# Gated recurrence of a hybrid trunk layer: score products of 32 columns, state products of 64 value columns, one output bank for two heads

## The chip, the core and the metric

The kernel runs on one core of a Trainium2 chip. The core's engines run side by side, each through its own list of instructions in order: PE (TensorE, matrix products; its weight loads are listed as PEld), DVE (VectorE), ACT (ScalarE), POOL (GpSimd) and SP, which issues the DMAs. The metric is the device time of one execution in microseconds (us). The time before is 3231.66 us, the median of three runs (3231.03 to 3231.88).

## What is computed

One layer: an RMS norm, a combined input projection, a gated linear recurrence (branch A), a pooling branch (branch B), their gated merge, an output projection, and a gated MLP. There are 2048 tokens behind 16 meta tokens, 1024 features and 8 heads; a head has 128 key features and 64 value features. All of it is float32. The change touches the recurrence alone:

```python
def hgrn2_mixer(q, f_logit, i, og, lb, head_g):
    """S_t = diag(f_t) S_{t-1} + (1 - f_t) i_t^T ; o_t = S_t^T q_t   (per head, S in R^{A_KDIM x A_VDIM})."""
    ...
    f = lbf + (1.0 - lbf) * jax.nn.sigmoid(f_logit.astype(f32))
    k = 1.0 - f
    ...
        o_inter = jnp.einsum('bhtk,bhkv->bhtv', q_ * jnp.exp(a_), S)
        scores = jnp.einsum('bhtsk,bhsk->bhts', q_[:, :, :, None, :] * decay, k_)
        o = o_inter + jnp.einsum('bhts,bhsv->bhtv', scores, v_)
        S = jnp.exp(a_last[:, :, 0, :])[..., None] * S + jnp.einsum(
            'bhsk,bhsv->bhkv', k_ * jnp.exp(a_last - a_), v_)
```

The kernel uses chunks of 128 tokens instead of the 64 of this code; the results are the same function.

## The kernel before

The tokens are taken in four segments of 512; the first has the 16 meta tokens ahead. A segment runs through the recurrence, the pooling branch, the norm factors of the heads, the out gate, the merge, the output projection, the second norm and the MLP. Weights come from memory in pieces of 512 KB; ACT (L85) and DVE (L86) split each piece into two parts, and a projection (`proj`, L108) makes three products of every 128 features with them, 24 products of up to 512 columns for one block of 128 output features.

The recurrence goes over four pairs of heads (`for p in range(PAIRS)`). For a pair, both heads lie side by side in the tiles `f`, `k` and `q` (features on partitions, tokens along the columns). Four projections fill them: two for `f` (sigmoid on ACT, L479 and L480, then `k` by L482), two for `q` (ACT L488, DVE L489). `decays` (DVE, L259, L273, L279) makes products of `f` within blocks of eight tokens. `all_scores` then fills the causal score tiles `at`, one per head, level by level: within blocks of 8, then between the halves of blocks of 16, 32, 64 and 128 tokens (`h_` = 0, 8, 16, 32, 64). Ahead of every level DVE multiplies `q` and `k` by decays, so PE, which reads both, has to be done with a level before DVE goes on to the next, and PE has to wait for DVE before it starts that one.

The three low levels (`h_` below 32) are whole products of 128 keys by 128 queries per chunk and head (L296), four chunks to a bank `sp`. Levels 0 and 8 are taken out of the bank by DVE with a mask, `copy_predicated` (L303), level 16 by ACT in four small copies per head (L300). Levels 32 and 64 (L309) compute only the needed blocks, 32 by 32 and 64 by 64, and ACT copies them (L312). At level 32 each head's products are written in the order `for o in range(0, C, 2 * h_): for c in range(n)`: four with their output on partitions 0 to 31, then four on partitions 64 to 95. The partitions of the output are the columns of the PE array that a product uses, and its column group is meant by that below.

`chunks_out` (per head) transposes the four chunks of `k` (L361, bank `ktp`; ACT copies to `kt`, L363), makes the state products (L366, bank `up`: weights `kt`, moving the 128 value columns of the pair, of which the head needs 64), updates the states on DVE (L372, L384), and sums scores times values (L378) and queries times state (L380) in bank `op`, all 128 value columns for each head; ACT copies the head's 64 rows out (L386). All banks of this part (`sp`, `ktp`, `up`, `op`) share three PSUM buffers (tag `hg`).

A scheduler sets the order of each engine's list ahead of time. It has placed products of the next pair's projections (L108) between the levels of the present pair, to fill the time in which DVE works on `q` and `k`. A fp32 product of the recurrence is listed in the trace as two records of weight load and product; L108, whose operands are split, has one record per product.

Of the kernel before, what the change touches and what calls it, by code (L numbers as in the profile page):

```python
# [16 lines left out]
P = 128  # L17
D = 1024
KB = D // P
META = 16  # L20
# [16 lines left out]
LEVELS = (8,)  # L37
# [7 lines left out]
def trunk_layer(ctx: ExitStack, tc: tile.TileContext, x, meta, wts, cst, gf, wpool, out):  # L45
# [14 lines left out]
    # ---------------------------------------------------------------- first loads  # L60
# [14 lines left out]
    # ---------------------------------------------------------------- helpers  # L75
    nxt = [0]

    def weights(lo=None):
        """the next piece of the weight stream, split exactly into two float32r parts"""
        i = nxt[0]  # L80
        nxt[0] += 1
        raw = wpl.tile([P, 1024], F32, name="raw", bufs=RAW)
        nc.sync.dma_start(out=raw, in_=wts[i])
        w = wpl.tile([P, 2, 1024], F32R, name="w")
        A.copy(out=w[:, 0, :], in_=raw)  # L85
        (lo or V).tensor_tensor(out=w[:, 1, :], in0=raw, in1=w[:, 0, :].bitcast(F32), op=ALU.subtract)  # L86
        return w

    def split(dst, src, scale=None):
        """dst[:,0] + dst[:,1] == src * scale"""  # L90
# [10 lines left out]
    def proj(w, kof, nk, src, c0, parts):  # L101
        """feature-major product: out[128 features, tokens]; one bank per part"""
# [11 lines left out]
    def rows_one_by_one(src, chunks, nk, consume):  # L114
        """the same with all weights held and chunk after chunk finished"""
# [10 lines left out]
    def rows_product(src, chunks, nk, consume, between=(), lo=None):  # L126
        """token-major product: out[tokens, 512]; the weights come in pieces of two k blocks"""
# [15 lines left out]
    def rsqrt(dst, src, t1, t2):  # L143
        """dst = (src) ** -0.5; src, t1, t2 in SBUF, float32; dst, t1, t2 written"""
# [7 lines left out]
    def square_sums(acc, src, m):  # L152
        """acc[:m, 0] = the sums of squares along src's rows of 512"""
# [3 lines left out]
    def inv_rms(ss, n):  # L157
        """ss [P, 2, n]: sums of squares of two half rows; returns [P, n], 1 / rms of the row"""
# [13 lines left out]
    def transposed(rows, sizes, offs, dst, gbase):  # L172
        """dst[kb] = the rows' block kb transposed, times its norm weight, split"""
# [36 lines left out]
    def norm1_first(xt, sizes, offs):  # L210
        """the first segment's, in two batches of rows"""
# [19 lines left out]
    def norm1(s):  # L231
        """closures, one per chunk of segment s, and the tiles that they fill"""
# [28 lines left out]
    def decays(f, N):  # L261
        """what the decays of blocks of eight need: the products around the middle of a block, their inverses"""
# [24 lines left out]
    def scores(q, k, geo, h_):  # L287
        """the scores between the halves of blocks of 2 h_ tokens (h_ 0: within blocks of eight)"""
        for (off, n, C, a_t) in geo:
            if h_ >= C:  # L290
                continue
            qv, kv = q[:, off:off + n * C], k[:, off:off + n * C]
            sp = ps.tile([P, 512], F32, name="sp", tag="hg", bufs=HG)
            if h_ < 32:
                for c in range(n):
                    T.matmul(sp[:C, c * C:(c + 1) * C], lhsT=kv[:, c * C:(c + 1) * C], rhs=qv[:, c * C:(c + 1) * C],  # L296
                             start=True, stop=True)
                if h_ == 16:
                    for o in range(0, C, 2 * h_):
                        A.copy(out=a_t[o:o + h_, :, o + h_:o + 2 * h_],  # L300
                               in_=sp[o:o + h_, :n * C].rearrange("p (c t) -> p c t", t=C)[:, :, o + h_:o + 2 * h_])
                    continue
                V.copy_predicated(out=a_t.rearrange("p c t -> p (c t)"),  # L303
                                  mask=masks[h_][:C, :n, :C].rearrange("p c t -> p (c t)"), data=sp[:C, :n * C])
                continue
            for o in range(0, C, 2 * h_):
                for c in range(n):
                    b = c * C + o
                    T.matmul(sp[o:o + h_, c * h_:(c + 1) * h_], lhsT=kv[:, b:b + h_], rhs=qv[:, b + h_:b + 2 * h_],  # L309
                             start=True, stop=True)  # L310
            for o in range(0, C, 2 * h_):
                A.copy(out=a_t[o:o + h_, :, o + h_:o + 2 * h_],  # L312
                       in_=sp[o:o + h_, :n * h_].rearrange("p (c t) -> p c t", t=h_))
# [40 lines left out]
    def chunks_out(h, q, k, tot, off, n, C, a_t, vt, first, o_raw, W):  # L354
        """the outputs of n chunks of C tokens at column off for head h, and the states between them"""
        p, r = h // 2, h % 2
        N = n * C
        qv, kv = q[:, off:off + N], k[:, off:off + N]
        ktp = ps.tile([P, 512], F32, name="ktp", tag="hg", bufs=HG)
        for c in range(n):  # L360
            T.transpose(out=ktp[:C, c * P:(c + 1) * P], in_=kv[:, c * C:(c + 1) * C], identity=ident)  # L361
        kt = tpl.tile([P, 512], F32, name="kt", tag="t")
        A.copy(out=kt[:C, :n * P], in_=ktp[:C, :n * P])  # L363
        up = ps.tile([P, 512], F32, name="up", tag="hg", bufs=HG)
        for c in range(n):
            T.matmul(up[:, c * P:(c + 1) * P], lhsT=kt[:C, c * P:(c + 1) * P], rhs=vt[c][:C, p * P:(p + 1) * P],  # L366
                     start=True, stop=True)
        if n > 1:
            sc = tpl.tile([P, 3, P], F32, name="sc", tag="t")
        states = [st[:, h, :]]  # L370
# [387 lines left out]
```

## Time and profile before

| what | value |
|---|---|
| median of 3 runs | 3231.66 us |
| profiled execution, span from first to last instruction | 3224.6 us |
| PE busy | 3162.8 us (98%) |
| DVE busy | 1761.0 us (55%) |
| ACT busy | 1154.1 us (36%) |
| products of the low score levels (L296, 128 columns) | 768 records, 101.1 us |
| products of levels 32 and 64 (L309) | 768 records, 34.6 us |
| granted TensorE clock, mean | 0.995 |

The span is the time from the first to the last instruction of the profiled execution; the median of the runs is 7.1 us longer. Busy times are sums over the whole span. Records of PE overlap each other (the mean record of L296 lasts 286 ns, but the next one starts after some 0.11 us), so what a group of products costs is read from the starts of what stands before and behind it. Where an engine stands idle ahead of an instruction, the trace gives the time in square brackets with what ended it.

### The profile page before, as it was taken

The page shows a single profiled execution, that of the slowest core. Times are in us where ns is not written, and L with a number is a line of the kernel's source. Part 1 is how long each engine was busy: PE and PEld are TensorE (multiplying, and loading weights), DVE is VectorE, ACT ScalarE, POOL GpSimd, SP SyncE. Part 2 cuts the span into 40 slices and gives each one's busy share as a digit, 9 for nine tenths or more (in the row PEclk, how much of TensorE's full clock was granted, in tenths as well). Part 3 has the DMA queues.
Part 4 walks back from the last instruction along what each step waited for, and adds up shares of the span by engine and source line. Part 5 has one row for each costly group of instructions (what it writes and reads, how often), then busy time and mean ns, then how long its engine had stood idle before and what let it go on. Part 6 is the DMA issues. An engine that isn't in the chain of part 4 may idle for free.

```text
span 3224.6 us, 41323 instructions
## 1 busy us (share of the span) xinstructions
PE 3162.8 (98%) x16748; PEld 2640.0 (82%) x16748; DVE 1761.0 (55%) x2959; ACT 1154.1 (36%) x1897; POOL 51.2 (2%) x183
## 2 busy tenths in 40 slices
PE   7999999999999999999999999999999999999998
PEld 6999978898878788888877778888888878878887
DVE  5776355454477636445457754654456783354545
ACT  4333244242333325323333433532333342232323
POOL 1000000000000000000000000000000000000000
PEclk9999999999999999999999999999999999999999
DMA  4112232222331223222241122322223112222222
GB/s 149 53 54 79 86 105 92 92 92 95 101 111 60 73 97 118 92 92 98 91 150 60 53 90 95 110 98 92 98 99 124 53 59 95 95 80 97 95 95 85
DMA packets 81730, 294.58 MB, mean 91 GB/s; under 512 B 9074, under 2 KB 9202, under 8 KB 81540
## 3 DMA queue, kind: packets, MB, share of 16 engines
q1 hardware_dynamic: 81540, 291.95, 27.1%
q8 instruction: 131, 2.15, 0.3%
q14 instruction: 59, 0.48, 0.0%
HBM read 283.52 MB, written 8.39 MB: 91 GB/s over the span
## 4 chain that ended last, share of the span: by engine, by line
PE 92%; DVE 6%; ACT 1%; issue 0%; DMA 0%; SPq 0%; DVEq 0%; ACTq 0%
PE pt L108 60%; PE rp L137 23%; PE sp L296 3%; DVE q L259 1%; DVE scr L259 1%; PE up L366 1%; PE tp L185 1%; DVE k L259 1%; PE sp L309 1%; PE op L380 1%; PE op L378 1%; DVE w L86 1%; PE ktp L361 0%; DVE q L489 0%; PE pp L504 0%
## 5 line engine op out<-in xcount | busy, mean ns | idle before, releaser
L108 PE MATMUL pt<-z,w 128*128 128x512 f32 (+3 forms) x9552 | 1945.8, 362 | 0.0
L108 PEld LDWEIGHTS pt<-z,w 128*128 128x128 f32 x9552 | 1594.1, 188 | 291.6 <-issue 7.5
L86 DVE TENSOR_TENSOR w<-raw,w 128x1024 fp32r<-128x1024 f32 x500 | 612.2, 1224 | 1070.2 <-ACT w L85 1063.5
L85 ACT CAST w<-raw 128x1024 fp32r<-128x1024 f32 x504 | 528.1, 1048 | 753.9 <-PE rp L137 358.7
L137 PE MATMUL rp<-w,act 128*128 128x512 f32 x2040 | 474.4, 394 | 0.0
L137 PEld LDWEIGHTS rp<-w,act 128*128 128x128 f32 x2040 | 383.4, 188 | 89.1
L137 PE MATMUL rp<-w,mix 128*128 128x512 f32 (+1 forms) x816 | 192.7, 395 | 0.0
L639 ACT COPY ub<-pt 128x512 f32<-128x512 f32 (+1 forms) x110 | 55.4, 503 | 354.8 <-PE pt L108 354.8
L137 PEld LDWEIGHTS rp<-w,mix 128*128 128x128 f32 (+1 forms) x816 | 147.6, 182 | 39.3 <-issue 3.5
L646 DVE SCALAR_TENSOR_TENSOR cv<-ub,cs,cv 128x512 f32<-128x512 f32 x176 | 131.7, 748 | 3.1
L581 ACT ACTIVATE sg<-pt 128x512 f32<-128x512 f32 (+1 forms) x80 | 41.2, 515 | 242.2 <-PE pt L108 242.2
L296 PE MATMUL sp<-q,k 128*128 128x128 f32 (+1 forms) x800 | 102.6, 282 | 24.2 <-DVE q L259 24.2
L296 PEld LDWEIGHTS sp<-q,k 128*128 128x128 f32 (+1 forms) x800 | 95.2, 194 | 36.1 <-issue 32.2
L649 ACT ACTIVATE sg<-cv 128x512 f32<-128x512 f32 x88 | 55.6, 632 | 178.5 <-DVE cv L646 178.5
L137 PE MATMUL rp<-w,z 128*128 128x512 f32 (+1 forms) x408 | 102.1, 402 | 0.0
L108 PE MATMUL pt<-oa,w 128*128 128x512 f32 (+2 forms) x480 | 95.0, 349 | 0.0
L108 PE MATMUL pt<-ob,w 128*128 128x512 f32 (+2 forms) x480 | 95.0, 349 | 0.0
L650 DVE TENSOR_TENSOR cv<-cv,sg 128x512 f32<-128x512 f32 x88 | 61.0, 693 | 61.5 <-ACT sg L649 61.5
L137 PEld LDWEIGHTS rp<-w,z 128*128 128x128 f32 (+1 forms) x408 | 73.8, 183 | 18.3 <-issue 0.4
L108 PEld LDWEIGHTS pt<-oa,w 128*128 128x128 f32 x480 | 77.9, 189 | 12.5
L108 PEld LDWEIGHTS pt<-ob,w 128*128 128x128 f32 x480 | 77.8, 189 | 12.5
L681 DVE TENSOR_TENSOR h<-h,rp 128x512 f32<-128x512 f32 x96 | 66.0, 688 | 29.1 <-PE rp L137 26.7
(159 smaller groups left out, 2107.6 us busy)
## 6 DMA issues: line engine op xcount, KB each, us to landing
raw<-in_wts_dram SPq DMA_DIRECT2D x504, 512.0 KB, 3.3
xt<-in_x_dram SPq DMA_DIRECT2D x16, 512.0 KB, 4.4
h<-in_x_dram SPq DMA_DIRECT2D x16, 512.0 KB, 4.5
out_dram<-h SPq DMA_DIRECT2D x12, 512.0 KB, 2.8
gfb<-in_gf_dram SPq DMA_DIRECT2D x8, 256.0 KB, 4.3
out_dram<-h SPq DMA_DIRECT2D x8, 256.0 KB, 2.0
wp<-in_wpool_dram SPq DMA_DIRECT2D x1, 256.0 KB
cs<-in_cst_dram SPq DMA_DIRECT2D x1, 68.0 KB, 6.8
```

The costliest lines, as they stand in the source:

```text
L85: A.copy(out=w[:, 0, :], in_=raw)
L86: (lo or V).tensor_tensor(out=w[:, 1, :], in0=raw, in1=w[:, 0, :].bitcast(F32), op=ALU.subtract)
L108: T.matmul(pt[:, :n], lhsT=w[:, wi, (kof + k) * P:(kof + k + 1) * P], rhs=src[k][:, xi, c0 + o:c0 + o + n], start=(k == 0 and i == 0), sto ...
L137: T.matmul(banks[ci][:n, :], lhsT=src[k][:, xi, o:o + n], rhs=w[:, wi, (k % 2) * 512:(k % 2 + 1) * 512], start=(k == 0 and i == 0), stop=( ...
L259: mul = lambda o, a, b: V.tensor_tensor(out=o, in0=a, in1=b, op=ALU.mult)
L296: T.matmul(sp[:C, c * C:(c + 1) * C], lhsT=kv[:, c * C:(c + 1) * C], rhs=qv[:, c * C:(c + 1) * C], start=True, stop=True)
L581: A.activation(out=sg[:, o:o + n], in_=pt[:, :n], func=AF.Sigmoid)
L639: A.copy(out=ub[:, 2 - e0 + o:2 - e0 + o + n], in_=pt[:, :n])
L646: V.scalar_tensor_tensor(out=cv, in0=ub[:, t_:t_ + SEG], scalar=col(C_CW + t_ * NF, j), in1=cv, op0=ALU.mult, op1=ALU.add)
L649: A.activation(out=sg, in_=cv, func=AF.Sigmoid)
L650: V.tensor_tensor(out=cv, in0=cv, in1=sg, op=ALU.mult)
L681: V.tensor_tensor(out=v, in0=v, in1=bank, op=ALU.add)
```

## The change

Level 16 joins the levels that go through a mask, and all three low levels are computed as blocks of 32 keys by 32 queries only (`B = 32`), of both heads into one bank: 32 products per level and pair, written so that consecutive products go to output partitions 0, 32, 64 and 96 in turn. DVE copies each level by its mask into a new tile `bt` that holds only the diagonal blocks (256 columns for the pair); behind level 16, ACT moves `bt` into `at` in four copies. Levels 32 and 64 also put both heads in one bank, with the chunk loop outside the block loop, and half as many ACT copies of twice the size.

`chunks_out` now takes a pair: both heads are transposed first, the state products have 64 moving columns and share one bank, the states are kept 64 columns wide, and the outputs of head 0 and head 1 go to partitions 0 to 63 and 64 to 127 of one bank, with weights of 64 columns; one ACT copy takes the whole bank. `at` has one tile per pair. The set-up makes three masks of 256 columns per partition instead of two of 512.

```diff
-LEVELS = (8,)
+LEVELS = (8, 16)
...
     def scores(q, k, geo, h_):
-        for (off, n, C, a_t) in geo:
+        for (off, n, C, W, a_t, b_t) in geo:
...
             if h_ < 32:
-                for c in range(n):
-                    T.matmul(sp[:C, c * C:(c + 1) * C], lhsT=kv[:, c * C:(c + 1) * C], rhs=qv[:, c * C:(c + 1) * C],
-                             start=True, stop=True)
-                if h_ == 16:
-                    for o in range(0, C, 2 * h_):
-                        A.copy(out=a_t[o:o + h_, :, o + h_:o + 2 * h_],
-                               in_=sp[o:o + h_, :n * C].rearrange("p (c t) -> p c t", t=C)[:, :, o + h_:o + 2 * h_])
-                    continue
-                V.copy_predicated(out=a_t.rearrange("p c t -> p (c t)"),
-                                  mask=masks[h_][:C, :n, :C].rearrange("p c t -> p (c t)"), data=sp[:C, :n * C])
-                continue
+                B = min(C, 32)
+                spv = sp[:C, :2 * n * B].rearrange("p (e c t) -> p e c t", e=2, c=n)
+                for e in range(2):
+                    for c in range(n):
+                        for o in range(0, C, B):
+                            x = slice(e * W + off + c * C + o, e * W + off + c * C + o + B)
+                            T.matmul(spv[o:o + B, e, c, :], lhsT=k[:, x], rhs=q[:, x], start=True, stop=True)
+                V.copy_predicated(out=b_t, mask=masks[h_, C], data=sp[:C, :2 * n * B])
+                if h_ == 16:
+                    for o in range(0, C, B):
+                        A.copy(out=a_t[o:o + B].rearrange("p e c t -> p (e c) t")[:, :, o:o + B],
+                               in_=b_t[o:o + B].rearrange("p (c t) -> p c t", t=B))
+                continue
+            spv = sp[:, :2 * n * h_].rearrange("p (e c t) -> p e c t", e=2, c=n)
+            for e in range(2):
+                for c in range(n):
+                    for o in range(0, C, 2 * h_):
+                        x = e * W + off + c * C + o
+                        T.matmul(spv[o:o + h_, e, c, :], lhsT=k[:, x:x + h_], rhs=q[:, x + h_:x + 2 * h_],
+                                 start=True, stop=True)
...
-    def chunks_out(h, q, k, tot, off, n, C, a_t, vt, first, o_raw, W):
+    def chunks_out(p, q, k, tot, geo, vt, first, o_raw):
...
+        for e in range(2):
+            v0 = p * P + e * VD
+            for c in range(n):
+                T.matmul(upv[:, e, c, :], lhsT=kts[e][:C, c * P:(c + 1) * P], rhs=vt[c][:C, v0:v0 + VD],
+                         start=True, stop=True)
...
         for c in range(n):
-            o_ = op[:, c * C:(c + 1) * C]
-            T.matmul(o_, lhsT=vt[c][:C, p * P:(p + 1) * P], rhs=a_t[:, c, :], start=True, stop=first)
+            for e in range(2):
+                v0 = p * P + e * VD
+                T.matmul(op[e * VD:(e + 1) * VD, c * C:(c + 1) * C], lhsT=vt[c][:C, v0:v0 + VD],
+                         rhs=a_t[:, e, c, :], start=True, stop=first)
             if not first:
-                T.matmul(o_, lhsT=states[c], rhs=qv[:, c * C:(c + 1) * C], start=False, stop=True)
+                for e in range(2):
+                    x = e * W + off + c * C
+                    T.matmul(op[e * VD:(e + 1) * VD, c * C:(c + 1) * C], lhsT=states[e][c], rhs=q[:, x:x + C],
+                             start=False, stop=True)
...
-        A.copy(out=o_raw[r * VD:(r + 1) * VD, off - r * W:off - r * W + N], in_=op[r * VD:(r + 1) * VD, :N])
+        A.copy(out=o_raw[:, off:off + N], in_=op[:, :N])
```

The scheduler's order moves with it. PE, first pair of the second segment, from level 16 to level 32, before:

```order
L296 MATMUL sp<-q,k 128x128 x8
L108 MATMUL pt<-z_4422,w 128x512
L108 MATMUL pt<-z_4423,w 128x512 x3
L108 MATMUL pt<-z_4424,w 128x512 x3
L309 MATMUL sp<-q,k 32x32 x16
```

and now (L300 are the 32 by 32 products of the low levels, L312 those of levels 32 and 64):

```order
L300 MATMUL sp<-q,k 32x32 x32
L108 MATMUL pt<-z_4625,w 128x512
L108 MATMUL pt<-z_4626,w 128x512 x3
L108 MATMUL pt<-z_4627,w 128x512 x3
L108 MATMUL pt<-z_4628,w 128x512
L312 MATMUL sp<-q,k 32x32 x16
```

Eight products of 128 by 128 have become 32 of 32 by 32, and eight projection products stand behind them instead of seven. PE, the same pair, from the transposes to the outputs, before (the second head follows in the same way):

```order
L361 MATMUL ktp<-ident,k 128x128 x4
L108 MATMUL pt<-z_4422,w 128x512 x3
L108 MATMUL pt<-z_4423,w 128x512
L366 MATMUL up<-vt,kt 128x128 x4
L378 MATMUL op<-at_465,vt 128x128
L380 MATMUL op<-q,st 128x128
L378 MATMUL op<-at_465,vt 128x128
L380 MATMUL op<-q,sc 128x128
```

and now (L366 the transposes, L375 the state products, L389 and L394 the outputs):

```order
L366 MATMUL ktp<-ident,k 128x128 x8
L108 MATMUL pt<-z_4625,w 128x512
L375 MATMUL up<-vt,kt 128x64 x8
L389 MATMUL op<-at_478,vt 64x128 x2
L394 MATMUL op<-q,st 64x128 x2
L389 MATMUL op<-at_478,vt 64x128 x2
L394 MATMUL op<-q,sc 64x128 x2
```

Both heads go through each step together; the outputs are twice as many products of half the weight columns, four per chunk. ACT, the same place and on to the next pair's `f` and `q`, before:

```order
L363 COPY kt<-ktp 128x512
L386 COPY oraw<-op 64x512
L363 COPY kt<-ktp 128x512
L479 ACTIVATE f<-pt,cs 128x512 x2
L480 ACTIVATE f<-f,lb 128x512 x2
L482 ACTIVATE k<-f,one 128x1024
L386 COPY oraw<-op 64x512
```

and now (L368 the copy of the transposes, L402 the copy of the outputs, L503 to L506 `f` and `k`):

```order
L368 COPY kt<-ktp 128x512 x2
L402 COPY oraw<-op 128x512
L503 ACTIVATE f<-pt,cs 128x512 x2
L504 ACTIVATE f<-f,lb 128x512 x2
L85 CAST w<-raw 128x1024
L506 ACTIVATE k<-f,one 128x1024
```

The next pair's `f` now stands behind the copy of both heads' outputs, where it stood behind that of the first head.

## Rows read from the trace of the kernel before

**Rows 1.** The page: busy times of the engines, and the chain's share by engine.

```profile
PE 3162.8 (98%) x16748; PEld 2640.0 (82%) x16748; DVE 1761.0 (55%) x2959; ACT 1154.1 (36%) x1897; POOL 51.2 (2%) x183
PE 92%; DVE 6%; ACT 1%; issue 0%; DMA 0%; SPq 0%; DVEq 0%; ACTq 0%
```

**Rows 2.** Busy time by stretch: length, PE, PEld, DVE, ACT, POOL, clock, DMA, GB/s.

```profile
880.00:1075.00 195.00, 187.43 (x1146) 154.40 (x1145) 145.77 (x292) 75.48 (x147) 3.31 (x8) 0.98 0.23 80
940.00:980.00 40.00, 36.96 (x242) 31.04 (x241) 31.91 (x71) 14.29 (x29) 0.00 (x0) 0.96 0.20 67
```

**Rows 3.** Waits, whole span: total us, times, longest.

```profile
PE sp L296 <- DVE q L259: 24.2, 16, 2.3
```

**Rows 4.** PE in time order, first pair of segment 2: start, length, instructions.

```profile
909.13 3.49 PE L108 MATMUL pt<-z,w 128*128 128x512 f32 x14
914.25 2.80 PE L108 MATMUL pt<-z,w 128*128 128x512 f32 x11
918.62 1.86 PE L108 MATMUL pt<-z,w 128*128 128x512 f32 x7
920.40 0.90 PE L309 MATMUL sp<-q,k 128*32 128x32 f32 x32
921.23 1.89 PE L108 MATMUL pt<-z,w 128*128 128x512 f32 x7
924.13 2.13 PE L108 MATMUL pt<-z,w 128*128 128x512 f32 x8
926.46 1.17 PE L108 MATMUL pt<-z,w 128*128 128x512 f32 x4
930.61 1.18 PE L108 MATMUL pt<-z,w 128*128 128x512 f32 x4
934.30 9.97 PE L108 MATMUL pt<-z,w 128*128 128x512 f32 x42
946.56 3.08 PE L296 MATMUL sp<-q,k 128*128 128x128 f32 x16 [2.29 <-DVE q L259]
```

**Rows 5.** The chain of waits in time order: start, length, instructions.

```profile
89.89 2.18 PE sp L296 x20
...
1298.75 88.76 PE pt L108 x384
```

**Rows 6.** Records of L309 begun by a window's end: PE and PEld counts.

```profile
920.30:920.54 0.24, 0.14 (x4) 0.14 (x5) 1.00 0.00 0
920.30:920.63 0.33, 0.23 (x9) 0.23 (x11) 1.00 0.00 0
920.30:920.84 0.54, 0.43 (x20) 0.44 (x21) 1.00 0.00 0
920.30:921.20 0.90, 0.80 (x32) 0.79 (x32) 1.00 0.00 0
...
923.00:923.32 0.32, 0.27 (x4) 0.27 (x5) 1.00 0.00 0
...
923.00:923.80 0.80, 0.74 (x12) 0.75 (x13) 1.00 0.00 0
```

**Rows 7.** Weight loads by shape: busy us, mean ns of one.

```profile
L366 PEld LDWEIGHTS up<-vt,kt 128*128 128x128 f32 x256 | 31.0, 191 | 5.3 <-ACT kt L363 4.9
L309 PEld LDWEIGHTS sp<-q,k 128*32 128x32 f32 x512 | 13.3, 112 | 5.8 <-issue 4.4 <-PE sp L296 0.8
```

**Rows 8.** DVE in time order, the same pair.

```profile
909.41 0.73 DVE L303 COPY_PREDICATED at<-mk,sp 128x512 f32<-128x512 uint8 x1 [0.16 <-PE sp L296]
...
911.16 1.22 DVE L259 TENSOR_TENSOR k<-k,scr 128x1024 f32<-128x1024 f32 x1
...
928.63 0.35 DVE L372 SCALAR_TENSOR_TENSOR sc<-st,tt,up 128x128 f32<-128x128 f32 x1 [2.84 <-issue]
...
934.24 0.72 DVE L259 TENSOR_TENSOR scr<-f 128x128 f32<-128x128 f32 x2
```

**Rows 9.** ACT in time order, the same pair.

```profile
931.41 1.26 ACT L479 ACTIVATE f<-pt,cs 128x512 f32<-128x512 f32 x2
```

More of the change, by code (lines that the diff above doesn't have):

```diff
@@ L352, in all_scores @@
         return [tot[:, e * NCH:(e + 1) * NCH] for e in range(2)]
-    def chunks_out(h, q, k, tot, off, n, C, a_t, vt, first, o_raw, W):
-        p, r = h // 2, h % 2
+    def chunks_out(p, q, k, tot, geo, vt, first, o_raw):
+        off, n, C, W, a_t, _ = geo
         N = n * C
[L358 to L363, printed above, removed]
-        up = ps.tile([P, 512], F32, name="up", tag="hg", bufs=HG)
-        for c in range(n):
-            T.matmul(up[:, c * P:(c + 1) * P], lhsT=kt[:C, c * P:(c + 1) * P], rhs=vt[c][:C, p * P:(p + 1) * P],
-                     start=True, stop=True)
+        kts = []
+        for e in range(2):
+            kv = k[:, e * W + off:e * W + off + N]
+            ktp = ps.tile([P, 512], F32, name="ktp", tag="hg", bufs=HG)
+            for c in range(n):
+                T.transpose(out=ktp[:C, c * P:(c + 1) * P], in_=kv[:, c * C:(c + 1) * C], identity=ident)
+            kt = tpl.tile([P, 512], F32, name="kt", tag="t")
+            A.copy(out=kt[:C, :n * P], in_=ktp[:C, :n * P])
+            kts.append(kt)
+        up = ps.tile([P, 512], F32, name="up", tag="hg", bufs=HG)
+        upv = up.rearrange("p (e c v) -> p e c v", e=2, v=VD)
+        for e in range(2):
[3 more added lines that the diff above has]
+                         start=True, stop=True)
@@ L381, in chunks_out @@
-        if first:
-            V.tensor_copy(out=st[:, h, :], in_=up[:, :P])
-        else:
-            V.scalar_tensor_tensor(out=st[:, h, :], in0=states[n - 1], scalar=tot[:, n - 1:n],
-                                   in1=up[:, (n - 1) * P:n * P], op0=ALU.mult, op1=ALU.add)
-        A.copy(out=o_raw[r * VD:(r + 1) * VD, off - r * W:off - r * W + N], in_=op[r * VD:(r + 1) * VD, :N])
+                for e in range(2):
+                    x = e * W + off + c * C
+                    T.matmul(op[e * VD:(e + 1) * VD, c * C:(c + 1) * C], lhsT=states[e][c], rhs=q[:, x:x + C],
+                             start=False, stop=True)
@@ L388, in trunk_layer @@
+        for e in range(2):
+            if first:
+                V.tensor_copy(out=st[:, 2 * p + e, :], in_=upv[:, e, 0, :])
+            else:
+                V.scalar_tensor_tensor(out=st[:, 2 * p + e, :], in0=states[e][n - 1], scalar=tot[e][:, n - 1:n],
+                                       in1=upv[:, e, n - 1, :], op0=ALU.mult, op1=ALU.add)
+        A.copy(out=o_raw[:, off:off + N], in_=op[:, :N])
     nxt[0] = V_AT
```

64 lines of the change are left out of this document (34 added, 30 removed).

## The prediction

> **What bounds the kernel now.** I read the page first: PE is busy 98% of the span and carries 92% of the chain that ended last; DVE carries 6% [rows 1]. A busy PE is not yet a bound, so the next view is the stretch that the change touches. In the recurrence of the second segment PE was busy 187.4 of 195 us and DVE 145.8 [rows 2]: PE is the limit there as well, DVE is second with a quarter of its time free. What PE lacks is mostly one wait, ahead of the first score level of each pair, for DVE's product on `q`: 24.2 us in 16 waits [rows 3]. So the time follows what PE has to do in the recurrence, as long as DVE stays ahead of it between the levels.
>
> What a block of small products costs PE is read from the projection products around it. 384 of them took 88.76 us [rows 5], 0.231 us each. In one pair [rows 4] the 14 that begin at 909.13 and the level 8 block behind them end at 914.25: 5.12 - 3.24 = 1.88 us for the block. Level 16: 914.25 to 918.62 less eleven, 1.83. I take 1.85 for each of the three low levels. Level 32 (16 products, 32 records): 918.62 to 921.23 less seven, 0.99. Transposes, state products and outputs of both heads: 924.13 to 934.30 less sixteen, 10.17 - 3.70 = 6.47 us for 56 records (8 + 16 + 32), 0.116 each.
>
> **The low score levels.** Each goes from 8 products of 128 columns to 32 of 32 columns, 16 records to 64. All hangs on what a record of 32 columns costs when the column group changes with every product. The block of level 32 shows it. Its first load begins at 920.40 [rows 4], and five loads have begun by 920.54: one in 30 ns or so. From 920.54 to 920.63 six more begin, two in 30 ns; then ten in 210 ns, so again some ticks with two [rows 6]. Each head writes four products (eight records) to partitions 0 to 31 and then eight records to partitions 64 to 95, so the group changes behind records 8, 16 and 24, and the doubled ticks lie around record 8. In the 64-column block behind it, which never changes group, loads come singly: eight in 0.48 us, 60 ns each [rows 6]. I read this as two column groups that run beside each other, each at 30 ns a record, for as long as PE looks ahead over the change. The three changes save some nine ticks of 32: 23 ticks are 0.7 us, and 0.99 - 0.72 leaves 0.27 us for entering and leaving such a block.
>
> In the new order every second record changes the group. With two groups at a time a record costs 15 ns: 64 x 0.015 + 0.27 = 1.23 us a level, 0.62 less than now, 1.86 for three levels. Bounds: four groups at a time, 7.5 ns, 0.75 us a level; single file, 30 ns, 2.19 us. I take 15 because exactly two are seen together. Level 32 gets the same alternation between two groups: 32 x 0.015 + 0.27 = 0.75 instead of 0.99, 0.24 less. Level 64 is left in one group: nothing.
>
> The Trainium skill (TensorE: Matmul & The Clock Gate, Part 1) says that start-to-start never drops below about 25 ns however small a product is. By that alone a level would take 64 x 0.025 + 0.27 = 1.87 us and the scores would gain nothing. Here the trace speaks against it, with 11 loads begun 0.23 us after the first [rows 4, 6]; as a rival it stands below.
>
> **State products and outputs.** The state products move 64 columns instead of 128 but still load 128 weight columns. The mean load lasts 191 ns with 128 columns and 112 with 32 [rows 7], 0.82 ns a column, so 128 columns occupy the load path for some 105 ns, which is what a record takes now. I cost this edit at nothing; if the moving columns set the pace, 16 records save at most half, 0.9 us a pair. The outputs are 32 records of 64 weight columns, alternating between two groups. Side by side at 0.116 per group they take 32 x 0.058 = 1.86 us; in single file 3.71. But outputs of a chunk wait for its state, and the states are now a DVE chain of six updates for both heads: 0.35 us each at 128 columns [rows 8], between 0.18 and 0.35 at 64; at 0.29 six are 1.75, with the lead into the first and the last chunk's records some 2.4 us. I take 2.4. With 24 other records at 0.116 (2.78), one more entry into a tiled block (0.27) and 0.1 for the wait on the `kt` copy, these steps come to 5.55 instead of 6.47: 0.92 less.
>
> **What lies beside PE.** DVE loses one copy of 512 columns (0.73 us) [rows 8] of four and has three of 256 left, between 0.37 and 0.73 each; ACT loses half its copies. Neither is the bound. The tight place is between levels: DVE's product on `k` ended at 912.38 [rows 8], and the level 8 block began at 914.25 - 1.85 = 912.40. PE will come 0.62 + 0.23 (13 projection products instead of 14) earlier, DVE some 0.9 (scores done 0.6 earlier, one narrow copy instead of two): no wait, or 0.4 if the copy stays at 0.73. Level 16 gains a copy ahead of DVE's next product, and the eighth projection product (0.23) stands against it. The additional mask work of the set-up, some 14 short DVE instructions of 0.36 (934.24 shows two in 0.72 [rows 8]), happens once while PE runs the first value product; I take nothing, 5 us if that cover fails.
>
> The wait ahead of the first level stays. In the first pair PE finishes the outputs at 934.30 and waits 2.29 us before 946.56 [rows 4]; DVE begins that pair's `decays` at 934.24, when ACT, which took `f` up at 931.41 behind the first head's output copy, has it ready [rows 8, 9]. In the new order `f` stands behind the copy for both heads, some 2 us later against the end of the outputs, while 50 projection products instead of 42 follow (1.85 us more for PE to do) and one weight split (L86) fewer stands in DVE's way. So the wait stays near 2.3, and moves forward with the outputs.
>
> **The sum.** Per pair 1.86 + 0.24 + 0.92 = 3.02 us; 12 pairs in three segments, 36.2. In the first segment the two meta products of a level made its block 2.18 us [rows 5], 0.33 more than 1.85, and are to cost 4 x 0.015 now: 0.27 on each of two levels, 3.56 a pair, 14.2 for four. Together 50.4. The profiled span of 3224.6 becomes 3174.2; the median of the runs lay 7.1 above the span, so 3181, 1.6% less. Four groups at a time would take off another 0.48 x 3 x 16 = 23 us, DVE updates at half price some 8: 3150 is the low end.
>
> **Rivals.**
>
> *Given back at the first level.* The time from the end of the outputs to the next pair's first level is a chain over ACT and DVE (oraw, `f`, `decays`, `q`), which no edit shortens. For it: the new place of `f` behind the copy of both heads. Against it: the additional projection products behind the outputs. If half of the pairs return what they gained, 8 x 3.02 = 24 us; and after such a wait of 2.29 us the block at 946.56 took 3.08 us instead of 1.85, in a stretch with the granted clock at 0.96 (part of it at 1.2 instead of 2.4 GHz) [rows 2, 4]: eight more of those are 10 us. 3204 to 3214.
>
> *A floor per record.* The 32 records of level 32 averaged 0.7 / 32 = 22 ns. If that is a floor of issue and not the mean of single and double ticks, a level is 64 x 0.022 + 0.27 = 1.68: 0.51 for three, level 32 nothing, outputs 0.92: 1.43 x 16 + 2 = 25 us, 3207. For it: no shorter mean is seen over any block. Against it: the doubled ticks. By the Trainium skill's 25 ns, named above, it would be the outputs' gain alone, about 3216.
>
> *Single file, the slower side.* If a change of group in every product stops PE from looking ahead, groups never overlap: 30 ns a record, 60 a product. A level is 2.19 (+0.34, three times), level 32 1.23 (+0.24), the outputs 3.71 (+0.39 with their entry): 1.65 a pair, 26 us in all less some 2 in the first segment: 3256. It decides from 49 ns a product, (1.85 - 0.27) / 32. Against it: the overlap at every change that the trace has. If only the low levels go in single file and the outputs overlap, it comes to about +0.3 a pair, 3235: no change.
>
> **How the numbers follow.** Forecast 0.60, given back 0.15, floor 0.09, scores alone in single file 0.06, all in single file 0.10. The first three end faster; a little of them falls inside 0.2% (6.5 us, about what a measurement of this kernel can tell from no change): faster 0.82, same 0.08, slower 0.10. The range runs from 3150 to 3214, which holds the forecast with its bounds, the waits given back and most of the floor.
>
> **What would show it.** Right: blocks of the low levels at about 1.2 us between projection products, with 64 records of 15 ns; outputs near 2.4 us and ended by DVE's state updates; state products at the old 0.11 a record; waits for `q` at about 24 us in all. Wrong: records at 22 ns or above, outputs at 3.7, a wait ahead of level 8, 16 or 32 in every pair, or waits at the first level well above 2.3 us with a lower granted clock behind them.

## The result and the profile after

The changed kernel takes 3142.11 us (median of four runs, 3138.75 to 3147.79) against 3231.77: a ratio of 0.9725, with a 95% interval from 0.9711 to 0.9738. The forecast was 3181 with a range from 3150 to 3214: the direction was right, the gain of 89.7 us was nearly twice the 50.4 us of the sum, and the time lies below the range. In the profiled executions the span went from 3224.6 to 3140.2 us, 84.4 less; the other 5 us are the difference between span and median, 7.1 us before and 1.9 now.

The page of the changed kernel, busy times and the share of the chain by engine (compare [rows 1]):

```profile
PE 3080.5 (98%) x19052; PEld 2552.0 (81%) x19052; DVE 1721.6 (55%) x2944; ACT 1136.8 (36%) x1765; POOL 48.9 (2%) x181
PE 92%; DVE 6%; ACT 1%; issue 0%; DMA 0%; SPq 0%; DVEq 0%; ACTq 0%
```

PE is still the bound and still 92% of the chain. It has 2304 records more and 82.3 us less to do. The wait that stood in [rows 3] keeps its total within 0.5 us. PE's waits over the whole span (total us, times, longest):

```profile
PE sp L300 <- DVE q L259: 24.7, 16, 2.1
```

PE in order of time, the first pair of the second segment (start, length, instructions, idle time before with its releaser), to be read against [rows 4]. L300 are the products of the low levels, L312 levels 32 and 64, L366 transposes, L375 state products, L389 and L394 outputs:

```profile
885.53 0.75 PE L300 MATMUL sp<-q,k 128*32 128x32 f32 x64 [1.39 <-DVE q L259]
886.21 3.28 PE L108 MATMUL pt<-z,w 128*128 128x512 f32 x13
889.42 0.76 PE L300 MATMUL sp<-q,k 128*32 128x32 f32 x64
890.11 3.04 PE L108 MATMUL pt<-z,w 128*128 128x512 f32 x12
...
893.78 2.12 PE L108 MATMUL pt<-z,w 128*128 128x512 f32 x8
895.83 0.70 PE L312 MATMUL sp<-q,k 128*32 128x32 f32 x32
896.46 1.89 PE L108 MATMUL pt<-z,w 128*128 128x512 f32 x7
...
899.35 1.90 PE L108 MATMUL pt<-z,w 128*128 128x512 f32 x7
...
902.36 2.00 PE L375 MATMUL up<-vt,kt 128*128 128x64 f32 x16
904.28 0.44 PE L389 MATMUL op<-at,vt 128*64 128x128 f32 x4
...
906.18 11.83 PE L108 MATMUL pt<-z,w 128*128 128x512 f32 x50
920.10 0.76 PE L300 MATMUL sp<-q,k 128*32 128x32 f32 x64 [2.09 <-DVE q L259]
```

With 0.231 us for each projection product, as in the prediction:

| block, us | before | predicted | after |
|---|---|---|---|
| a low level (886.21 to 890.11 less 13) | 1.85 | 1.23 | 0.90 |
| level 32 (893.78 to 896.46 less 7) | 0.99 | 0.75 | 0.83 |
| level 64 (896.46 to 899.35 less 7) | 1.27 | unchanged | 1.27 |
| transposes, state products, outputs (899.35 to 906.18 less 8) | 6.47 | 5.55 | 4.98 |
| of these the outputs (904.28 to 906.18) | | 2.4 | 1.90 |
| wait ahead of the next first level | 2.29 | near 2.3 | 2.09 |

The levels 8, 16 and 32 carry no wait in brackets. Whole pairs can be compared too, from one first level to the next, if the projection products are taken out, whose number differs. The windows below count only line L108 (stretch, length, PE busy with its count, PEld busy with its count, granted clock, DMA share, GB/s). Before, from the first pair to the second of segment 2, and from the second to the third of segments 3 and 2:

```profile
907.35:946.56 39.21, 24.49 (x97) 17.61 (x97) 1.00 0.16 55
1730.85:1769.36 38.51, 24.27 (x95) 17.16 (x95) 1.00 0.17 55
946.56:986.53 39.97, 24.90 (x95) 17.69 (x95) 0.96 0.17 53
```

and after, from the first pair to the second and from the second to the third of segment 2:

```profile
885.53:920.10 34.57, 24.53 (x98) 17.95 (x98) 1.00 0.14 47
920.10:952.92 32.82, 23.87 (x94) 17.19 (x94) 1.00 0.25 81
```

Less 0.231 us per projection product, the first interval goes from 39.21 - 22.42 = 16.79 to 34.57 - 22.65 = 11.92 us, 4.87 less; the second, at full clock in both, from 16.56 to 11.10, 5.46 less. The sum had 3.02. The row with a clock of 0.96 is the same work with a stretch at 1.2 instead of 2.4 GHz in it: 18.02 instead of 16.56, some 1.5 us. Such stretches lie at other places in every execution and make single spans uncertain by a few us.

### The profile page after: what moved, and what is told of

It reads as the page before. It is cut to its first block, busy times and chain, and to the rows that moved or that the text cites. A ratio compares the mean times of both kernels' runs of the same rounds, so it can differ in the third digit from the quotient of the medians.

```text
span 3140.2 us, 45714 instructions
## 1 busy us (share of the span) xinstructions
PE 3080.5 (98%) x19052; PEld 2552.0 (81%) x19052; DVE 1721.6 (55%) x2944; ACT 1136.8 (36%) x1765; POOL 48.9 (2%) x181
## 4 chain that ended last, share of the span: by engine, by line
PE 92%; DVE 6%; ACT 1%; issue 0%; DMA 0%; SPq 0%; DVEq 0%; ACTq 0%
PE pt L108 61%; PE rp L137 24%; PE sp L300 1%; PE up L375 1%; DVE q L259 1%; DVE scr L259 1%; PE sp L312 1%; PE tp L185 1%; DVE k L259 1%; DVE q L513 1%; DVE w L86 1%; PE op L389 1%; PE ktp L366 0%; PE op L394 0%; PE pp L527 0%
## 5 line engine op out<-in xcount | busy, mean ns | idle before, releaser
L108 PE MATMUL pt<-z,w 128*128 128x512 f32 (+3 forms) x9552 | 1939.0, 362 | 0.0
L108 PEld LDWEIGHTS pt<-z,w 128*128 128x128 f32 x9552 | 1596.3, 189 | 296.9 <-issue 10.7
L108 PE MATMUL pt<-oa,w 128*128 128x512 f32 (+2 forms) x480 | 95.1, 350 | 0.0
L108 PE MATMUL pt<-ob,w 128*128 128x512 f32 (+2 forms) x480 | 95.0, 350 | 0.0
L108 PEld LDWEIGHTS pt<-oa,w 128*128 128x128 f32 x480 | 77.9, 189 | 12.5
L108 PEld LDWEIGHTS pt<-ob,w 128*128 128x128 f32 x480 | 77.9, 189 | 12.5
L609 DVE TENSOR_TENSOR sg<-sg,pt 128x512 f32<-128x512 f32 (+1 forms) x80 | 46.5, 582 | 62.7 <-PE pt L108 62.6
L95 ACT ACTIVATE z<-tp,cs 128x128 fp32r<-128x128 f32 (+3 forms) x152 | 61.0, 438 | 29.9 <-PE tp L185 12.8
```

The source lines that it names most:

```text
L95: A.activation(out=dst[0], in_=src, func=AF.Copy, scale=scale)
L108: T.matmul(pt[:, :n], lhsT=w[:, wi, (kof + k) * P:(kof + k + 1) * P], rhs=src[k][:, xi, c0 + o:c0 + o + n], start=(k == 0 and i == 0), sto ...
L609: V.tensor_tensor(out=gates[i][:, o:o + n], in0=gates[i][:, o:o + n], in1=pt[:, :n], op=ALU.mult)
```

## Experiments

The theory (A in the expectations): PE works on products of different column groups side by side, as far as the order of the products lets it, and a low level costs what this overlap leaves. The rival (B): the gain is the fewer columns of the small products, whatever their order.

### The order of the low levels

Two kernels with the same 32 products per level in another order. Group by group:

```diff
-                for e in range(2):
-                    for c in range(n):
-                        for o in range(0, C, B):
+                for o in range(0, C, B):
+                    for e in range(2):
+                        for c in range(n):
```

> The changed kernel with the same 32 products of each low level in another order: all eight of output partitions 0 to 31 first, then those of 32 to 63, and so on, so that the column group changes three times in a block instead of 31. Theory A (products of different column groups run beside each other, those of one group follow at 30 ns a record): some 55 ticks of 30 ns, a level of 1.9 us instead of 0.90, 48 levels, +48 us: 3190 us. Rival B (the records are cheap because they are small, whatever group they go to): no change, 3142 us.

And groups 0 and 32 in alternation, then 64 and 96:

```diff
-                for e in range(2):
-                    for c in range(n):
-                        for o in range(0, C, B):
+                for o2 in range(0, C, 2 * B):
+                    for e in range(2):
+                        for c in range(n):
+                            for o in range(o2, min(C, o2 + 2 * B), B):
```

> The changed kernel with the 32 products of a low level alternating between output partitions 0 and 32 for the first half and between 64 and 96 for the second. Theory A with as many groups at a time as the order offers: 15 ns a record, 1.23 us a level, +0.33 for each of 48 levels, 16 us: 3158 us. If PE never runs more than two at a time and a record costs 10 ns for another reason, or by rival B: 3142 us.

Measured: 3194.34 us (ratio 0.9889, 0.9874 to 0.9903) and 3160.80 us (0.9783, 0.9768 to 0.9797). PE in order of time, the same place, group by group:

```profile
899.61 3.28 PE L108 MATMUL pt<-z,w 128*128 128x512 f32 x13
...
904.66 3.05 PE L108 MATMUL pt<-z,w 128*128 128x512 f32 x12
```

and with two groups:

```profile
889.91 3.28 PE L108 MATMUL pt<-z,w 128*128 128x512 f32 x13
...
894.17 3.05 PE L108 MATMUL pt<-z,w 128*128 128x512 f32 x12
```

The level block is 904.66 - 899.61 - 3.00 = 2.05 us group by group, 1.26 with two groups and 0.90 with four: the same products, columns and bytes. With 48 such blocks the differences are 48 x 1.15 = 55 and 48 x 0.36 = 17 us, and the times lie 52 and 19 us above the changed kernel. B is out. Group by group, the new products would have been dearer than the old ones of 128 columns (1.85).

### The price of a record by itself

0.90 us for 64 records could be three groups at a time (9.8 ns each and the 0.27 us for entering and leaving a block from the prediction) or four (7.5 ns each, and a dearer entry). Making every product twice, in each of the three orders, adds 64 records without a second entry:

```diff
-                for e in range(2):
+                for e in (0, 1, 0, 1):
```

> The changed kernel, but every product of the three low levels is made twice in a row of the same order (128 records a level and pair instead of 64; the second writing repeats the first). What is added is 64 records without a further entry or exit, so the growth of the block between projection products (0.90 us in the changed kernel) is the price of 64 records by itself. If three of the four groups run at a time (9.8 ns a record, entry and exit 0.27): 0.90 + 0.63 = 1.53 us. If all four do (7.5 ns, entry and exit then 0.42): 0.90 + 0.48 = 1.38 us. In time: 48 x 0.63 = 30 us more than 3142, or 48 x 0.48 = 23 us more, and what DVE's waits give back.

> As the last two, in the order that alternates two groups (block 1.26 us with 64 records). Two groups side by side at 15 ns a record: 1.26 + 0.96 = 2.22 us; time 48 x 0.96 = 46 us over that order's 3161.

> As the last, in the order group by group (block 2.05 us with 64 records). One group at 30 ns a record: 2.05 + 1.92 = 3.97 us. If 2.05 us holds an entry and exit of 0.27 as well, a record is 27.8 ns: 3.83 us. Time 48 x 1.9 = some 90 us over that order's 3194.

Measured: 3201.4, 3222.16 and 3300.72 us (one run each). PE in order of time, the 13 projection products ahead of a level's 128 records and those behind it, with four groups:

```profile
911.94 3.28 PE L108 MATMUL pt<-z,w 128*128 128x512 f32 x13
...
916.37 2.12 PE L108 MATMUL pt<-z,w 128*128 128x512 f32 x8
```

with two:

```profile
912.93 3.28 PE L108 MATMUL pt<-z,w 128*128 128x512 f32 x13
...
918.19 2.12 PE L108 MATMUL pt<-z,w 128*128 128x512 f32 x8
```

and with one:

```profile
930.75 3.28 PE L108 MATMUL pt<-z,w 128*128 128x512 f32 x13
...
937.83 2.12 PE L108 MATMUL pt<-z,w 128*128 128x512 f32 x8
```

| order | 64 records, us | 128 records, us | one record, ns | the rest of the block, us |
|---|---|---|---|---|
| group by group | 2.05 | 4.08 | 31.7 | 0.02 |
| two groups | 1.26 | 2.26 | 15.6 | 0.26 |
| four groups | 0.90 | 1.43 | 8.3 | 0.37 |

With one group and with two nearly all blocks outside the stretches at the lower clock agree to 0.03 us. With four, five of the 24 blocks at levels 8 and 16 of the last three segments read 1.43; the others read 1.59 us and more, most of them with a wait inside, so 8.3 ns is the price in an undisturbed block.

The price of a record falls as 1 : 2.0 : 3.8. All four groups run side by side, and what grows is the entry. Neither alternative was exact: the record is that of four groups, give or take 0.8 ns, and the entry lies between the two guesses.

The Trainium skill (TensorE: Matmul & The Clock Gate, Part 3) says that products on different column positions of the array run at the same time; this trace agrees, with 31.7 ns alone and 8.3 ns with four groups. The floor of some 25 ns from start to start that the Trainium skill gives in Part 1 of the same page doesn't hold across column groups here, by the same 8.3 ns.

The times with two and one group are 61 and 106 us above those of the single-product kernels; 48 x 1.00 and 48 x 2.03 would be 48 and 97. With four groups it is 59 instead of 48 x 0.53 = 25. With four groups and with two, PE has a new wait (PE's waits, the same columns as above, first four groups, then two):

```profile
PE sp L300 <- issue: 14.7, 10, 2.5
...
PE sp L301 <- issue: 8.4, 6, 1.8
```

"issue" is time in which PE waited for nothing that the profile shows. With one group there is none, and in the changed kernel it is 0.3 us. What makes it was not tested. With four groups PE also waits 3.1 us for DVE's product on `k`, in ten places.

### The outputs

Head by head instead of in alternation, all else as in the changed kernel:

```diff
-        for c in range(n):
-            for e in range(2):
+        for e in range(2):
+            for c in range(n):
...
-            if not first:
-                for e in range(2):
+                if not first:
```

> The changed kernel with the output products of head 0 (partitions 0 to 63) all ahead of those of head 1 (64 to 127), instead of in turn. Theory A: the two halves overlap only at the one change, so the outputs take some 3.5 us instead of 1.9, +1.6 for each of 16 pairs, 26 us: 3168 us. Rival B (64 weight columns are loaded in half the time): 3142 us. If the state updates on DVE had set the pace of the outputs, head by head would be no slower either.

Measured: 3175.52 us (0.9825, 0.9809 to 0.9842). PE, the first of the output rows and what follows the last:

```profile
914.91 0.43 PE L389 MATMUL op<-at,vt 128*64 128x128 f32 x2
...
918.17 7.21 PE L108 MATMUL pt<-z,w 128*128 128x512 f32 x30
```

The outputs take 918.17 - 914.91 = 3.26 us instead of 1.90: 1.36 x 16 = 22 of the 33 us. The other 11 are not placed row by row. The granted clock was 0.992 or 0.993 in all four runs of this kernel and 0.994 to 0.998 in those of the changed kernel; in this execution it was 0.51 from 262 to 270 us, for one. Such stretches are part of the 11; why this kernel has more of them was not tested. In single file throughout, the prediction's price was 3.71 us: some overlap at the changes of group is left.

Then the other way about: the scores of the kernel before, with the transposes, state products and outputs of the changed kernel (its diff is that of `chunks_out` above).

> The kernel before with the changed step from the transposes to the outputs alone (both heads together, state products of 64 value columns, one output bank), and the scores as they were. By the two traces this step fell from 6.47 to 4.98 us a pair, 1.5 for 16 pairs, 24 us: 3208 us; the scores then account for some 66. If the saving comes mainly from the order in which the scheduler placed both heads' blocks, more than 24: 3195 us or less.

Measured: 3195.01 us (0.9887, 0.9872 to 0.9902). The step in this kernel:

```profile
916.98 2.13 PE L108 MATMUL pt<-z,w 128*128 128x512 f32 x8
...
924.05 6.28 PE L108 MATMUL pt<-z,w 128*128 128x512 f32 x26
```

924.05 - 916.98 less nine projection products is 4.99 us, as in the changed kernel, 1.48 less than before: 24 of 37 us, and 3208 by the block alone. More is to be found in the second pair of a segment, which the prediction never looked at. PE before, the outputs of the first head there:

```profile
1748.14 2.35 PE L108 MATMUL pt<-z,w 128*128 128x512 f32 x9
...
1754.43 0.49 PE L380 MATMUL op<-q,sc 128*128 128x128 f32 x2 [0.75 <-DVE sc L372]
...
1761.14 7.42 PE L108 MATMUL pt<-z,w 128*128 128x512 f32 x31
```

With 23 projection products within (9 + 4 + 5 + 5) the step was 13.00 - 5.32 = 7.68 us in this pair, not 6.47: PE waited 0.75 us for a state. That wait is gone. Some 10 of this kernel's 37 us have no row; its runs spread from 3191 to 3199.

The expected 3208 was missed by 13 us, and the time lies at the bound that had been set for the scheduler's order; what that order brings by itself was not tested. Pair by pair, net of projection products, the four recurrences are 30.5 us shorter than before, of 34.5 between the two spans. From this kernel to the changed one it is 52.9 us, so the scores account for some 53 of the whole gain, not for the 66 of the expectation.

### State products

They move all 128 value columns again, one bank per head:

```diff
-        up = ps.tile([P, 512], F32, name="up", tag="hg", bufs=HG)
-        upv = up.rearrange("p (e c v) -> p e c v", e=2, v=VD)
+        ups = []
...
+            up = ps.tile([P, 512], F32, name="up", tag="hg", bufs=HG)
...
-                T.matmul(upv[:, e, c, :], lhsT=kts[e][:C, c * P:(c + 1) * P], rhs=vt[c][:C, v0:v0 + VD],
+                T.matmul(up[:, c * P:(c + 1) * P], lhsT=kts[e][:C, c * P:(c + 1) * P], rhs=vt[c][:C, p * P:(p + 1) * P],
```

> The changed kernel, but the state products move all 128 value columns of the pair again, one bank per head, and the updates read the head's 64 columns out of it. In the changed kernel 16 such records lie between 902.36 and 904.28 us, 0.12 us each, no less than with 128 columns before. Theory A (the load of 128 weight columns sets their pace, so halving the moving columns brought nothing): same time, 3142 us, within 4. Rival (the moving columns set the pace, and 0.12 us is a floor reached for another reason): a record of 128 columns costs more, up to twice, 16 x 0.05 to 16 x 0.12 = 0.8 to 1.9 us a pair, 3155 to 3172 us.

Measured: 3146.17 us (0.974, 0.9726 to 0.9754; the interval overlaps that of the changed kernel). The 16 records and the output behind them:

```profile
907.46 2.05 PE L374 MATMUL up<-vt,kt 128*128 128x128 f32 x16
909.44 0.44 PE L389 MATMUL op<-at,vt 128*64 128x128 f32 x4
```

1.98 us against 1.92 with 64 columns: 0.06 x 16 = 1 us of the 4 by which the median is longer. The moving columns don't set the pace.

### Level 64 in two groups

The one level that the change left in a single group:

```diff
+            if h_ == 64:
+                for c in range(n):
+                    for e in range(2):
+                        x = e * W + off + c * C
+                        T.matmul(sp[e * h_:(e + 1) * h_, c * h_:(c + 1) * h_], lhsT=k[:, x:x + h_],
+                                 rhs=q[:, x + h_:x + 2 * h_], start=True, stop=True)
+                for e in range(2):
+                    A.copy(out=a_t[:h_, e, :, h_:], in_=sp[e * h_:(e + 1) * h_, :n * h_].rearrange("p (c t) -> p c t", t=h_))
+                continue
```

> The changed kernel, but at level 64 the products of the second head go to output partitions 64 to 127 and alternate with those of the first head (ACT then takes the bank in two copies). In the changed kernel this level is the one that never leaves a column group: 16 records in 1.27 us. Theory A (two groups side by side in alternation halve the time of a record): 16 x 0.03 to 16 x 0.04 + 0.27 = 0.75 to 0.9 us, 0.4 to 0.5 less a pair, 6 to 8 us in all, 3134 to 3136. Rival (a 64 by 64 product gains nothing, or the added ACT copy delays what follows): 3142 or a little above.

Measured: 3138.96 us (0.9717, 0.9703 to 0.973). PE, the projection products ahead of level 64 and behind it:

```profile
899.74 1.89 PE L108 MATMUL pt<-z,w 128*128 128x512 f32 x7
...
902.17 2.36 PE L108 MATMUL pt<-z,w 128*128 128x512 f32 x9
```

The block is 0.81 us instead of 1.27, as expected, and the pair from 888.81 to 923.44 us, net of its 100 projection products, is 34.63 - 23.11 = 11.52 us instead of 11.92; the next pair is 0.48 less. In the median only 3.2 us of the 7 show, and the interval overlaps that of the changed kernel: the gain is shown in the trace, not in the time. This execution had a stretch at the lower clock between 193 and 262 us (0.97, where the changed kernel's had 1.00), and the runs of one kernel differ by as much as the effect.

### The wait ahead of the first level

DVE in the changed kernel: the last state updates of the pair and the beginning of the next pair's `decays`; then ACT at the same place:

```profile
904.39 0.47 DVE L382 SCALAR_TENSOR_TENSOR sc<-st,tt,up 128x64 f32<-128x64 f32 x2 [3.54 <-PE up L375]
...
905.55 0.47 DVE L400 SCALAR_TENSOR_TENSOR st<-sc,tt,up 128x64 f32<-128x64 f32 x2
909.51 0.76 DVE L259 TENSOR_TENSOR scr<-f 128x128 f32<-128x128 f32 x2 [3.49 <-ACT f L504]
```

```profile
906.32 0.59 ACT L402 COPY oraw<-op 128x512 f32<-128x512 f32 x1 [3.53 <-PE op L394]
906.80 1.27 ACT L503 ACTIVATE f<-pt,cs 128x512 f32<-128x512 f32 x2
```

DVE stands idle for 3.49 us until `f` is there, ACT for 3.53 us until the last output is, and `f` is behind it on ACT though its projections were done. So the copy goes to DVE:

```diff
-        A.copy(out=o_raw[:, off:off + N], in_=op[:, :N])
+        V.tensor_copy(out=o_raw[:, off:off + N], in_=op[:, :N])
```

> The changed kernel, but the copy of the output bank is made by DVE instead of ACT. In the changed kernel ACT waits 3.5 us for the last output product, copies the bank, and takes up the next pair's f only then (906.80 us), DVE's decays begin at 909.51, and the next pair's first score level waits 2.1 us at 920.10 for what DVE makes out of them. Theory (this order on ACT is what the wait ahead of the first level hangs on): f is taken up before the outputs are done, the decays begin some 2.7 us earlier, and the first level waits for nothing in the second and the last pair of a segment: 12 us less, and some of the stretches at the lower clock behind those waits go with it: 3126 to 3131 us. Rival (DVE is late anyway, its own queue sets the wait): 3142, or some us more for the copy on DVE.

Measured: 3135.47 us (0.9707, 0.9693 to 0.9721). The interval overlaps that of the changed kernel, but the slowest of the four runs (3137.41) lies below the fastest there (3138.75). DVE and PE in this kernel:

```profile
910.88 0.69 DVE L402 COPY oraw<-op 128x512 f32<-128x512 f32 x1 [0.31 <-PE op L394]
911.49 0.73 DVE L259 TENSOR_TENSOR scr<-f 128x128 f32<-128x128 f32 x2
...
916.21 0.69 DVE L513 TENSOR_TENSOR q<-pt,q 128x512 f32<-128x512 f32 x1 [0.47 <-ACT q L512]
```

```profile
910.74 11.60 PE L108 MATMUL pt<-z,w 128*128 128x512 f32 x49
923.27 0.75 PE L300 MATMUL sp<-q,k 128*32 128x32 f32 x64 [0.94 <-DVE tt L259]
```

`decays` begins 0.75 us behind the outputs (910.74) instead of 3.33. The wait fell from 2.09 to 0.94 us, though, not to zero: from 911.49 on DVE has one gap of 0.47 us until the level's operands are ready. So the order on ACT was about half of it. The other half is DVE's, but not its work alone, as the rival had it: `decays` now stands behind the copy on DVE, which waits 0.31 us for the last output and holds DVE for 0.61, while `f` had been done on ACT since 909.92. No kernel had the copy further back, so what is left for DVE's work by itself stays open. All waits ahead of first levels went from 24.7 to 18.0 us, 6.7 less, and the time is 6.6 less.

Both edits together:

> Both of the last two edits: the second head's level 64 products alternate with the first head's on the other half of the partitions, and DVE copies the output bank. If the two gains add up: some 20 us less than the changed kernel, 3120 to 3124. If PE, once the level is shorter, only waits longer for DVE: the gain of the copy alone, 3126 to 3131; if neither works, 3142.

Measured: 3127.96 us (median of five runs, 0.9682, 0.9668 to 0.9695), 14.2 us below the changed kernel, an interval that doesn't touch its own, and faster than both kernels of this case. The first level of the second pair, and the windows of L108:

```profile
923.51 0.76 PE L300 MATMUL sp<-q,k 128*32 128x32 f32 x64 [0.55 <-DVE q L259]
```

```profile
890.93:923.51 32.58, 24.53 (x98) 17.92 (x98) 1.00 0.16 50
923.51:955.91 32.40, 23.89 (x94) 17.10 (x94) 1.00 0.26 82
```

Net of projection products the pairs take 9.94 and 10.69 us, 2.0 and 0.4 less than in the changed kernel. The third and fourth pair do much the same, 4.9 us for a segment and 14.7 for three. 14.2 is more than the 3.2 and 6.6 of the two edits, by about the spread of the runs; it is less than the 18 to 22 us that were expected where the gains add up.

## Why the prediction was too small

**The mechanism was right for the scores, not for the outputs.** PE was the bound and stayed it; consecutive products on different output partitions overlap; the order is what pays. The waits at the first level stayed in sum (24.7 us for the predicted 24), those of the second and fourth pairs of the later segments at 2.09 us, no wait came up ahead of the levels 8, 16 and 32, and the state products gained nothing. The three kernels with another order came out slower than the changed one, the two of the scores by what their blocks in the trace say (52 for 55 us, 19 for 17), and the rivals did not happen: no floor at 22 ns, no single file, and at the first level something was given back in the first segment alone (below).

**The step that failed first: "I take 15 because exactly two are seen together."** The block of level 32 [rows 4, 6] has only two column groups in it, so it could show no more than two at a time. It bounded the overlap from below and was read as its size. With four groups in alternation a record costs 8.3 ns; a level took 0.90 us instead of 1.23, 0.33 x 48 = 16 us. The 15 ns were right for what they had been read from: with two groups the block was 1.26 us for the predicted 1.23. The bound with four groups, 0.75 us, had the record right and the entry too small: 0.27 us is the price with two groups, with four it is 0.37. The range had put "another 0.48 x 3 x 16 = 23 us" at its low end as something that four groups would give; 16 of them came.

**The second: the outputs at 2.4 us, set by a DVE chain of six updates at 0.29.** The six updates with 64 columns begin at 904.39 and the two for `st` at 905.55, 1.16 us for six, 0.19 each and near the lower bound of 0.18. No output waits for one: they take 1.90 us, which is the price side by side (1.86) that the prediction had worked out and set aside. The step as a whole was 4.98 instead of 5.55 us, 0.57 x 16 = 9 us.

**The third: all pairs priced by the first.** In the second pair of a segment the same step took 7.68 us before, not 6.47, with a wait for a state in the outputs. After the change it takes 5.33 us there (934.52 to 941.93 less nine projection products). It saves 2.35 instead of 1.49 us: 0.86 for each of three segments, 2.6 us.

**Smaller ones.** Level 32 came to 0.83, not 0.75: 1.3 us the other way. Its border there is dearer than 0.27, as 32 x 0.0156 = 0.50 leaves 0.33. The median of the runs lay 1.9 us above the profiled span, not 7.1: 5.2 us. Nearly every run on record lies some 1.8 us above its own span (1.7 to 2.8), so the 7.1 came from a profiled execution before that was some 5 us faster than the median: this part is chance. Together with the three above this is 16 + 9 + 2.6 - 1.3 + 5.2 = 31.5 of the 38.9 us between 3181 and 3142. The other 7 are placed in part. Pair by pair, net of projection products, the four recurrences of the two traces differ by 80.7 of the 84.4 us between the spans, 30.3 more than the 50.4 of the sum; the terms above are 26.3 of these, and six waits that became 0.2 us shorter are another 1.3. Some 4 us lie outside the recurrences. Stretches at the lower clock, some 1.4 us each, that lie elsewhere in the two executions are some of the rest.

**The first segment.** It was priced at 3.56 us a pair. PE there, the first rows of the second and third pair's first level, before:

```profile
125.89 1.34 PE L296 MATMUL sp<-q,k 128*16 128x16 f32 x12 [0.84 <-DVE q L259]
...
167.96 1.34 PE L296 MATMUL sp<-q,k 128*16 128x16 f32 x12 [0.84 <-DVE q L259]
```

and after:

```profile
120.13 0.84 PE L300 MATMUL sp<-q,k 128*16 128x16 f32 x68 [1.42 <-DVE q L259]
...
156.74 0.84 PE L300 MATMUL sp<-q,k 128*16 128x16 f32 x68 [1.43 <-DVE q L259]
```

With 192 projection products on both sides the pair went from 42.07 to 36.61 us, 5.46 less, although the wait rose by 0.6 us. So three pairs did give 1.8 us back at the first level; that the waits still add up to the predicted 24 is luck in part, as six others fell by 0.2 each. The whole segment gained some 21 us for the 14.2 forecast. The 0.33 us for a level's meta products was misread: it sets the length of a row, 2.18 us, against a cost between starts, 1.85; between starts the same 20 records take 2.00 us (89.82 to 91.82).

**The place of `f` on ACT.** The prediction saw that `f` would stand behind the copy of both heads' outputs, and that the additional projection products would cover it, so that the wait stays. It did, but it was not the least that the wait could be: one copy moved to DVE gave 6.6 us.

## What to carry to other kernels

Where small products with at most 32 output columns follow each other on PE, write them so that consecutive ones go to output partitions 0, 32, 64 and 96 in turn: the order alone was worth 52 us here, and in the order group by group 32 products of 32 columns cost more than eight of 128. A block in the old trace shows an overlap only as far as it has groups to overlap; take its price as a bound and put the range out to what four would give. If a wait on an engine that isn't the bound stays after a change, look at what stands ahead of the releasing instruction in that engine's list: here it was a copy that another engine could make.

## What the runs showed of the hardware

- A record of a 32 by 32 product in float32 cost 31.7 ns in one column group, 15.6 with two in alternation and 8.3 with four. Entering and leaving the block cost next to nothing with one group (0.02 us), 0.26 with two and 0.37 with four. That the entry grows was not expected.
- State products with 128 weight columns cost 0.12 us a record whether 64 or 128 columns move (1.92 and 1.98 us for 16).
- With 128 records of 8.3 ns in a row PE showed waits on "issue", up to 2.5 us, ten times in the span (14.7 us), and with 128 of 15.6 ns six times (8.4 us). With 128 of 31.7 ns it showed none, with 64 of 8.3 ns 0.3 us in all.
- The same wait of 2.09 us at the first level was followed by 14 projection products in 3.51 us in one pair (from 920.78 us in the changed kernel) and in 5.00 us in another (from 988.22). The granted clock of the pair was 1.00 in the first and 0.92 in the second.
